# A two-block transformer in fp32 on one core: recombined feed-forward products with an addition done by DMA, unscaled rows at two norms, and another order of the chunks

## The chip, the cores and the metric

One core of one Trainium2 chip runs the whole program. The metric is the device time of one execution in microseconds (us). Before the change it is 2960.03 us, the median of three runs (2956.86 to 2961.02). A difference of about 0.2% (6 us) is what a measurement of this kernel can tell from none.

## What is computed

256 tokens of width 2048 go through two blocks, everything in fp32. The first has differential attention and a gated recurrence, cross attention, and a gated feed-forward part; the second has a pooling mixer and gated linear attention, and again a gated feed-forward part. The change lies in the two feed-forward parts, which are alike (5632 hidden columns):

```
def rms_norm(x, g):
    y = x * lax.rsqrt(jnp.mean(x * x, axis=-1, keepdims=True) + NORM_EPS)
    return y * g

h = rms_norm(x, ffn_pre_g)
gate, up = jnp.split(h @ w_ffn_in, 2, axis=-1)          # 2048 x 5632 each
x = x + rms_norm((silu(gate) * up) @ w_ffn_out, ffn_post_g)
```

The outputs must agree with this in fp32.

## The kernel before

**Weights.** The weights come from memory once, on SP's queue: `slab` (L378) loads two k-tiles of 128 rows by 512 columns, 512 KB, into one of six `raw` buffers. `parts` turns a slab into two reduced-precision halves that TensorE takes at full speed: ScalarE (ACT) casts it to `wh` (L386), VectorE (DVE) writes the rest `wl = raw - wh` (L387). There are eight pairs of such buffers. The activations h are held transposed in high and low parts as well, so a product is three matmuls per k-tile: high by high, high by low, low by high. The 256 tokens are two token tiles.

**A feed-forward part** has 11 hidden chunks of 512 columns, and `FF_ORDER` says in which order they run. `(c, False)` is a *plain* chunk: a group of matmuls for gate and one for up, 192 matmuls in all. `(c, True)` is a *fast* chunk (`seven`): gate and up of both token tiles as the four blocks of a matrix product that is done with seven block products instead of eight (P1, Q3, Q5, Q7, P2, Q6, Q4), 168 matmuls. It has four steps `s`. A step loads four slabs (x, b12, b22, b21), makes four sums of slabs on DVE (L490, L493, L495, L500) and splits seven things, so it has eleven DVE instructions of 128x1024 and seven casts on ACT, and gives TensorE 42 matmuls. The sums of h that the products need come from `combos` (8 additions L456, 8 further ones, and a split each, L449 on ACT and L450 on DVE); in the kernel before, these are spawned behind the first plain chunk, and so run at the start of the first fast one. After the last step the seven banks are combined (L512 to L519), then Silu and the product follow, and a transposition. `(a, b)` is a *down* stage: the hidden chunks a to b-1 times the down weights; all but the last one write partial sums through ACT (`yp`) and GpSimd's (POOL) DMA to `y_part` (L1065), the second and later ones accumulating there (L1067).

**The norm ahead of it** (`normed`, with `scaled=True` in both feed-forward parts): four sums of squares of a token tile's row, the reciprocal root, four scaled copies `xn` (L338), and only then the transposes (L309) and splits (L327, L328).

**The order.** Each engine runs its own queue in program order; the program places every instruction by a priority. Slabs and splits of a fast chunk go ahead by `SLAB_AHEAD` 70, the combining by `POST_AHEAD` 150; spawned work (norms, combos, transposes) is dealt out between the matmuls.

Of the kernel before, what the change touches and what calls it, by code (L numbers as in the profile page):

```python
# [41 lines left out]
FF_ORDER = ((0, False), (1, True), (0, 2), (2, True), (3, False), (4, True), (2, 5),  # L42
            (5, True), (6, False), (7, True), (5, 8), (8, True), (9, False), (10, True), (8, 11))
# [43 lines left out]
class Builder:  # L87
# [391 lines left out]
    def seven(self, Wa, Wb, c0, S, consume):  # L479
# [3 lines left out]
        bank = {n: self.psmm() if i < 4 else self.ps("mm7") for i, n in enumerate(("P1", "Q3", "Q5", "Q7", "P2", "Q6", "Q4"))}  # L483
        for s in range(4):
            with self.tc.high_priority(offset=max(0, min(SLAB_AHEAD, self.tc.cur_priority - self.base))):
                w = {}
                x = self.slab(Wa, 2 * s, c0)
                w["P1"] = self.parts(x)
                b12 = self.slab(Wb, 2 * s, c0)
                nc.vector.tensor_tensor(x, x, b12, ALU.add)  # L490
                b22 = self.slab(Wb, 8 + 2 * s, c0)
                w["Q3"] = self.parts(b22)
                nc.vector.tensor_tensor(b12, b12, b22, ALU.add)  # L493
                w["Q5"] = self.parts(x)
                nc.vector.tensor_tensor(x, x, b22, ALU.add)  # L495
                w["Q7"] = self.parts(b12)
                b21 = self.slab(Wa, 8 + 2 * s, c0)
                w["P2"] = self.parts(b21)
                w["Q6"] = self.parts(x)
                nc.vector.tensor_tensor(x, x, b21, ALU.add)  # L500
                w["Q4"] = self.parts(x)
            for n, (wh, wl) in w.items():
# [6 lines left out]
                self.tick()  # L509
        with self.tc.high_priority(offset=POST_AHEAD):  # L510
# [23 lines left out]
    def normed(self, start, pre, scaled=False):  # L534
# [5 lines left out]
        def job(t):  # L540
            self.bound = True
            if scaled:
                acc, xs = self.small(4, "acc"), []
                for j, u in enumerate(start(t)):
                    self.square_sum(u, acc[:, j:j + 1])
                    xs.append(u)
                s = self.small(1, "ssq")
                self.nc.vector.tensor_reduce(s, acc, AX.X, ALU.add)
                r = self.rsqrt_mean(s, D)
                for j in range(4):  # L550
                    u = self.unit(name="xn")
                    self.scaled_copy(u, xs[j], r)
                    xs[j] = u
            else:
                xs = list(start(t))
# [8 lines left out]
            if scaled:  # L564
                rstd[t] = r
                return
# [43 lines left out]
    def boundary(self, start, pre, scaled=False):  # L610
# [8 lines left out]
        rstd, hT, job = self.normed(first, pre, scaled)  # L619
        return xs, rstd, hT, job  # L620
# [240 lines left out]
    def block1(self, x_src):  # L861
# [120 lines left out]
        _, _, hT, job = self.boundary(self.spilled(done, xd), "ffn_pre_g", True)  # L982
# [8 lines left out]
        return self.ffn(xd, hT, W[:, :HID], W[:, HID:], A["w_ffn_out"][0], A["ffn_post_g"][0])  # L991
# [12 lines left out]
    def ffn(self, xd, hT, Wg, Wu, Wd, post):  # L1004
# [8 lines left out]
        def run(job):  # L1013
# [7 lines left out]
            def plain(c):  # L1021
                sg = [None] * NT
# [55 lines left out]
            for a, b in FF_ORDER:  # L1078
                if b is True:
                    fast(a)  # L1080
                elif b is False:
                    plain(a)
                    if S is None:
                        S, more = self.combos(hT)
                        self.spawn(more)
# [5 lines left out]
    def block2(self, ffn1):  # L1091
# [219 lines left out]
```

## Time and profile before

| | before |
| --- | --- |
| median of three runs | 2960.03 us |
| the profiled execution, its own time | 2953.59 us |
| its span (first to last instruction) | 2951.8 us |
| TensorE busy | 2811.8 us (95%) |
| DVE busy | 2132.8 us (72%) |
| ACT busy | 1602.5 us (54%) |
| the 14 fast stages together | 683.9 us |
| the other stages of the feed-forward parts | for example 44.6 to 46.2 us for a plain chunk |

A stage here is the stretch from TensorE's first matmul of a chunk to its last. In a fast stage TensorE waits again and again, in a plain one hardly. "Busy" of TensorE is modelled from pipelined matmuls: a 512-column matmul shows 0.39 us, but the next one starts 0.2257 us later.

### The profile page before, as it was taken

To read this page: it belongs to the slowest core of one execution; us is meant where nothing else is said; L and a number is where in the kernel's file an instruction comes from. 1 tells how busy PE (TensorE), PEld (TensorE's weight loads), DVE (VectorE), ACT (ScalarE), POOL (GpSimd) and SP (SyncE) were. 2 spreads that over 40 slices of the span, in tenths; PEclk is the share of its full clock that TensorE was granted. 3 is DMA by queue.
4 is the path that set the end of the run, shared out by engine and by line. 5 is a ranking of instruction groups with operands and counts; after the bars stand their busy time and mean duration, and the time that the engine had idled before them with its cause. 6 is when DMAs were issued, how large, how long until landed. Compare 5 with 4: busy or idle time off the path is not lost. (4 is left out here: it accounts for less than half of the span.)

```text
span 2951.8 us, 35680 instructions
## 1 busy us (share of the span) xinstructions
PE 2811.8 (95%) x12860; PEld 2287.3 (77%) x12860; DVE 2132.8 (72%) x2669; ACT 1602.5 (54%) x2342; POOL 98.7 (3%) x169
## 2 busy tenths in 40 slices
PE   8999999987999999999999999999988999999998
PEld 6788888875787777778888998888875777777777
DVE  7666685679887886887665575555569887887886
ACT  6555675675555545555555474444465555555553
POOL 1000000000000000000000000000000000000000
PEclk9999999999999999999999999999999999999999
DMA  8555555554557657657655556666654657557655
GB/s 254 171 175 160 178 176 176 169 167 143 191 190 238 168 168 229 218 184 247 206 154 162 153 169 205 200 195 219 202 168 125 207 193 229 158 186 233 198 189 183
DMA packets 285682, 556.16 MB, mean 188 GB/s; under 512 B 19049, under 2 KB 30949, under 8 KB 285504
## 3 DMA queue, kind: packets, MB, share of 16 engines
q1 hardware_dynamic: 271344, 516.89, 55.4%
q0 software_dynamic: 13584, 35.93, 4.8%
q8 instruction: 101, 1.65, 0.2%
q10 hardware_dynamic: 576, 1.05, 0.1%
q14 instruction: 77, 0.63, 0.1%
HBM read 531.25 MB, written 22.54 MB: 188 GB/s over the span
## 5 line engine op out<-in xcount | busy, mean ns | idle before, releaser
L387 DVE TENSOR_TENSOR wl<-raw,wh 128x1024 fp32r<-128x1024 f32 (+1 forms) x1136 | 1364.4, 1215 | 631.4 <-ACT wh L386 623.3
L386 ACT CAST wh<-raw 128x1024 fp32r<-128x1024 f32 (+1 forms) x1136 | 1170.6, 1046 | 1046.5 <-PE mm L418 580.5
L418 PE MATMUL mm<-wh,hi 128*128 128x512 f32 (+2 forms) x2608 | 827.2, 394 | 13.6 <-ACT wh L386 13.5
L418 PE MATMUL mm<-wl,hi 128*128 128x512 f32 (+2 forms) x2608 | 807.1, 389 | 0.9 <-DVE wl L387 0.9
L418 PE MATMUL mm<-wh,lo 128*128 128x512 f32 (+2 forms) x2608 | 803.5, 388 | 0.0
L418 PEld LDWEIGHTS mm<-wh,hi 128*128 128x128 f32 x2608 | 482.8, 188 | 114.6 <-ACT wh L386 17.9
L418 PEld LDWEIGHTS mm<-wh,lo 128*128 128x128 f32 x2608 | 489.3, 188 | 98.9 <-issue 0.2
L418 PEld LDWEIGHTS mm<-wl,hi 128*128 128x128 f32 x2608 | 488.4, 188 | 99.4 <-DVE wl L387 3.6
L506 PE MATMUL mm<-wh,sh 128*128 128x512 f32 x448 | 182.3, 407 | 48.1 <-ACT wh L386 30.4
L508 PE MATMUL mm<-wh,sl 128*128 128x512 f32 x448 | 175.9, 393 | 0.7 <-DVE sl L450 0.7
L507 PE MATMUL mm<-wl,sh 128*128 128x512 f32 x448 | 175.8, 392 | 0.0
L506 PE MATMUL mm<-wh,hi 128*128 128x512 f32 x336 | 137.2, 408 | 30.4 <-ACT wh L386 30.4
L506 PEld LDWEIGHTS mm<-wh,sh 128*128 128x128 f32 x448 | 84.5, 189 | 85.2 <-ACT wh L386 50.0
L507 PE MATMUL mm<-wl,hi 128*128 128x512 f32 x336 | 134.8, 401 | 3.0 <-DVE wl L387 2.9
L508 PE MATMUL mm<-wh,lo 128*128 128x512 f32 x336 | 132.7, 395 | 0.0
L433 PE MATMUL mm<-wh,hi 128*128 128x512 f32 (+1 forms) x304 | 121.4, 399 | 4.3 <-ACT hi L327 4.2
L435 PE MATMUL mm<-wh,lo 128*128 128x512 f32 (+1 forms) x304 | 119.2, 392 | 0.0
L434 PE MATMUL mm<-wl,hi 128*128 128x512 f32 (+1 forms) x304 | 119.2, 392 | 0.0
L506 PEld LDWEIGHTS mm<-wh,hi 128*128 128x128 f32 x336 | 63.8, 190 | 59.0 <-ACT wh L386 46.8
L508 PEld LDWEIGHTS mm<-wh,sl 128*128 128x128 f32 x448 | 84.6, 189 | 20.3 <-DVE sl L450 2.8
L507 PEld LDWEIGHTS mm<-wl,sh 128*128 128x128 f32 x448 | 84.7, 189 | 17.8
L328 DVE SCALAR_TENSOR_TENSOR lo<-tp,vec,hi 128x128 fp32r<-128x128 f32 x224 | 68.6, 345 | 20.9 <-ACT hi L327 20.1
(287 smaller groups left out, 2259.0 us busy)
## 6 DMA issues: line engine op xcount, KB each, us to landing
raw<-w_in SPq DMA_DIRECT2D x256, 512.0 KB, 3.7
raw<-w_ffn_in SPq DMA_DIRECT2D x176, 512.0 KB, 4.4
raw<-w_ffn_out SPq DMA_DIRECT2D x88, 512.0 KB, 5.4
raw<-w_ffn_gate SPq DMA_DIRECT2D x88, 512.0 KB, 4.3
raw<-w_ffn_up SPq DMA_DIRECT2D x88, 512.0 KB, 4.6
raw<-w_ffn_down SPq DMA_DIRECT2D x88, 512.0 KB, 5.4
raw<-w_out SPq DMA_DIRECT2D x64, 512.0 KB, 4.2
raw<-w_branch_b SPq DMA_DIRECT2D x32, 512.0 KB, 3.8
```

Of the source, the lines that this page charges most:

```text
L328: nc.vector.scalar_tensor_tensor(lo[:, i, :], ps[:, i, :], g, hi[:, i, :].bitcast(F32), ALU.mult, ALU.subtract)
L386: nc.scalar.copy(hi[:, :, :ncol], raw[:, :, :ncol])
L387: nc.vector.tensor_tensor(lo[:, :, :ncol], raw[:, :, :ncol], hi[:, :, :ncol].bitcast(F32), ALU.subtract)
L418: nc.tensor.matmul(ps[t][:, :ncol], hT[t][kk // 4][p][:, kk % 4, :], w[:, i, :ncol], start=kk == first and p == 0 and w is wh, stop=kk == ...
L433: nc.tensor.matmul(ps[:, :ncol], xh, wh[:, i, :ncol], start=kk == first, stop=False)
L434: nc.tensor.matmul(ps[:, :ncol], xh, wl[:, i, :ncol], start=False, stop=False)
L435: nc.tensor.matmul(ps[:, :ncol], xl, wh[:, i, :ncol], start=False, stop=kk == last)
L506: nc.tensor.matmul(bank[n], xh, wh[:, i, :], start=kk == 0, stop=False)
L507: nc.tensor.matmul(bank[n], xh, wl[:, i, :], start=False, stop=False)
L508: nc.tensor.matmul(bank[n], xl, wh[:, i, :], start=False, stop=kk == 7)
```

## The change

There are five things. **One**, in a fast step the addition b12 + b22 is no longer a DVE instruction but an accumulating DMA on POOL's queue from one SBUF buffer into another (512 KB); the other three sums stay on DVE (L511, L515, L517), and Q4's operand is now formed in b21's buffer. **Two**, the next step's x is loaded and split before Q4 of this one, and the products run in the order P1, Q3, Q5, P2, Q6, Q7, Q4. **Three**, the rows at the two feed-forward norms are transposed unscaled; the statistics are made afterwards, and the factor `rstd` is applied to the products, as Silu's scale and in a `scalar_tensor_tensor`. **Four**, `combos` is spawned between the gate and the up group of the first plain chunk, and two plain chunks run first. **Five**, `FF_ORDER`: still four plain and seven fast chunks, but five down stages in place of four, one of them of a single chunk, `(8, 9)`.

```diff
-FF_ORDER = ((0, False), (1, True), (0, 2), (2, True), (3, False), (4, True), (2, 5),
-            (5, True), (6, False), (7, True), (5, 8), (8, True), (9, False), (10, True), (8, 11))
+FF_ORDER = ((0, False), (1, False), (2, True), (0, 3), (3, True), (4, False), (5, True), (3, 6),
+            (6, True), (7, False), (8, True), (6, 8), (9, True), (8, 9), (10, True), (9, 11))
...
-        for s in range(4):
-            with self.tc.high_priority(offset=max(0, min(SLAB_AHEAD, self.tc.cur_priority - self.base))):
-                w = {}
-                x = self.slab(Wa, 2 * s, c0)
-                w["P1"] = self.parts(x)
-                b12 = self.slab(Wb, 2 * s, c0)
-                nc.vector.tensor_tensor(x, x, b12, ALU.add)
-                b22 = self.slab(Wb, 8 + 2 * s, c0)
-                w["Q3"] = self.parts(b22)
-                nc.vector.tensor_tensor(b12, b12, b22, ALU.add)
-                w["Q5"] = self.parts(x)
-                nc.vector.tensor_tensor(x, x, b22, ALU.add)
-                w["Q7"] = self.parts(b12)
-                b21 = self.slab(Wa, 8 + 2 * s, c0)
-                w["P2"] = self.parts(b21)
-                w["Q6"] = self.parts(x)
-                nc.vector.tensor_tensor(x, x, b21, ALU.add)
-                w["Q4"] = self.parts(x)
...
+        def early(s):
+            x = self.slab(Wa, 2 * s, c0)
+            return x, self.parts(x)
...
+        with ahead():
+            x, p1 = early(0)
+        for s in range(4):
+            with ahead():
+                w = {"P1": p1}
+                b12 = self.slab(Wb, 2 * s, c0)
+                b22 = self.slab(Wb, 8 + 2 * s, c0)
+                b21 = self.slab(Wa, 8 + 2 * s, c0)
+                nc.vector.tensor_tensor(x, x, b12, ALU.add)
+                nc.gpsimd.dma_start(b12, b22, accum_op=ALU.add)
+                w["Q3"] = self.parts(b22)
+                w["Q5"] = self.parts(x)
+                nc.vector.tensor_tensor(x, x, b22, ALU.add)
+                w["P2"] = self.parts(b21)
+                nc.vector.tensor_tensor(b21, b21, x, ALU.add)
+                w["Q6"] = self.parts(x)
+                w["Q7"] = self.parts(b12)
+                if s < 3:
+                    x, p1 = early(s + 1)
+                w["Q4"] = self.parts(b21)
+            products(s, ("P1", "Q3", "Q5", "P2", "Q6", "Q7", "Q4"), w)
...
-            if scaled:
-                acc, xs = self.small(4, "acc"), []
-                for j, u in enumerate(start(t)):
-                    self.square_sum(u, acc[:, j:j + 1])
-                    xs.append(u)
-                s = self.small(1, "ssq")
-                self.nc.vector.tensor_reduce(s, acc, AX.X, ALU.add)
-                r = self.rsqrt_mean(s, D)
-                for j in range(4):
-                    u = self.unit(name="xn")
-                    self.scaled_copy(u, xs[j], r)
-                    xs[j] = u
-            else:
-                xs = list(start(t))
+            xs = list(start(t))
...
-                    nc.scalar.activation(sg[t], ps, AF.Silu)
+                    nc.scalar.activation(sg[t], ps, AF.Silu, scale=rstd[t])
...
-                    nc.vector.tensor_tensor(u, ps, sg[t], ALU.mult)
+                    nc.vector.scalar_tensor_tensor(u, ps, rstd[t], sg[t], ALU.mult, ALU.mult)
...
                 self.group(Wg, c * CW, hT, ks, g_in, apart=c == 0)
+                if c == 0:
+                    S, more = self.combos(hT)
+                    self.spawn(more)
                 self.group(Wu, c * CW, hT, ks, u_in)
...
-                            nc.scalar.activation(g, g, AF.Silu)
-                            nc.vector.tensor_tensor(u, u, g, ALU.mult)
+                            nc.scalar.activation(g, g, AF.Silu, scale=rstd[t])
+                            nc.vector.scalar_tensor_tensor(u, u, rstd[t], g, ALU.mult, ALU.mult)
```

**DVE in a fast step.** Before, a step in the middle of a fast chunk stands like this on DVE (L490 to L500 are the four additions, L387 the low parts; `raw_7615` is x, `raw_7621` b12, `raw_7624` b22, `raw_7640` b21):

```order
L490 TENSOR_TENSOR raw_7615<-raw_7615,raw_7621 128x1024
L493 TENSOR_TENSOR raw_7621<-raw_7621,raw_7624 128x1024
L387 TENSOR_TENSOR wl_7632<-raw_7615,wh_7631 128x1024
L387 TENSOR_TENSOR wl_7637<-raw_7621,wh_7636 128x1024
L495 TENSOR_TENSOR raw_7615<-raw_7615,raw_7624 128x1024
L387 TENSOR_TENSOR wl_7643<-raw_7640,wh_7642 128x1024
L387 TENSOR_TENSOR wl_7647<-raw_7615,wh_7646 128x1024
L500 TENSOR_TENSOR raw_7615<-raw_7615,raw_7640 128x1024
L387 TENSOR_TENSOR wl_7652<-raw_7615,wh_7651 128x1024
L387 TENSOR_TENSOR wl_7700<-raw_7697,wh_7699 128x1024
L387 TENSOR_TENSOR wl_7709<-raw_7706,wh_7708 128x1024
L490 TENSOR_TENSOR raw_7697<-raw_7697,raw_7703 128x1024
```

In the changed kernel the same place reads (x is `raw_7328`, b12 `raw_7380`, b22 `raw_7382`, b21 `raw_7384`, the next step's x `raw_7410`):

```order
L511 TENSOR_TENSOR raw_7328<-raw_7328,raw_7380 128x1024
L387 TENSOR_TENSOR wl_7389<-raw_7382,wh_7388 128x1024
L387 TENSOR_TENSOR wl_7393<-raw_7328,wh_7392 128x1024
L387 TENSOR_TENSOR wl_7398<-raw_7384,wh_7397 128x1024
L515 TENSOR_TENSOR raw_7328<-raw_7328,raw_7382 128x1024
L517 TENSOR_TENSOR raw_7384<-raw_7384,raw_7328 128x1024
L387 TENSOR_TENSOR wl_7403<-raw_7328,wh_7402 128x1024
L387 TENSOR_TENSOR wl_7407<-raw_7380,wh_7406 128x1024
L387 TENSOR_TENSOR wl_7413<-raw_7410,wh_7412 128x1024
L387 TENSOR_TENSOR wl_7417<-raw_7384,wh_7416 128x1024
L511 TENSOR_TENSOR raw_7410<-raw_7410,raw_7462 128x1024
```

There are ten instructions between two first additions in place of eleven; the low part of Q7 (`wl_7407`, of the buffer that the DMA adds into) stands as the eighth, and the next step's P1 and Q4 stand behind it.

**SP's and POOL's queues.** In the changed kernel SP issues the four slabs of a step and the next ones like this; DMASW in the list of waits is a transfer of POOL's queue:

```order
L378 DMA raw_7380<-w_ffn_in 128x2x512 [waits DMAHW3_49,DVE_49]
L378 DMA raw_7382<-w_ffn_in 128x2x512 [waits DMASW0_49,DMAHW0_49,DVE_49,Activation_49]
L378 DMA raw_7384<-w_ffn_in 128x2x512 [waits DMAHW5_49,DVE_49,Activation_49]
L378 DMA raw_7410<-w_ffn_in 128x2x512 [waits DMAHW6_49,DVE_49]
L378 DMA raw_7462<-w_ffn_in 128x2x512 [waits DMAHW7_49,DVE_49]
L378 DMA raw_7464<-w_ffn_in 128x2x512 [waits DMASW2_49,DMAHW4_49,DVE_49,Activation_49]
```

and POOL, where a fast chunk follows a down stage, like this (L512 is the addition by DMA, L1069 the accumulation into `y_part`):

```order
L512 DMA raw_8736<-raw_8738 128x1024 [waits DMAHW3_49,DMAHW4_49,DMAHW2_49,DMAHW5_49,DMAHW1_49,DMAHW7_49,DMASW6_49,DVE_49]
L1069 DMA y_part_5590<-yp_8717 128x512 [waits DMASW7_49,Activation_49]
L512 DMA raw_8818<-raw_8820 128x1024 [waits DMAHW1_49,DMAHW0_49,DMAHW7_49,DMASW0_49,DVE_49]
L1069 DMA y_part_5594<-yp_8720 128x512 [waits DMASW1_49,Activation_49]
L512 DMA raw_8900<-raw_8902 128x1024 [waits DMAHW3_49,DMAHW4_49,DMASW2_49,DVE_49]
```

The slab b22 of each step now waits for the addition by DMA of an earlier step, and the slabs behind it on SP with it; before, no slab waited for POOL's transfers there, and POOL's queue held only the rows of `y_part`.

**The sums of h on DVE.** Before, they stand among the additions of the first fast chunk:

```order
L456 TENSOR_TENSOR sv_5994<-hi_5711,lo_5712 128x512
L456 TENSOR_TENSOR sv_5996<-hi_5753,lo_5754 128x512
L387 TENSOR_TENSOR wl_6160<-raw_6157,wh_6159 128x1024
L318 TENSOR_TENSOR lo_6009<-tp_5998,hi_6008 128x512
L318 TENSOR_TENSOR lo_6013<-tp_6003,hi_6012 128x512
L463 TENSOR_TENSOR sv_5996<-sv_5994,sv_5996 128x512
L490 TENSOR_TENSOR raw_6157<-raw_6157,raw_6163 128x1024
```

Now they stand among the low parts of the plain chunks' weights:

```order
L456 TENSOR_TENSOR sv_5828<-hi_5677,lo_5678 128x512
L456 TENSOR_TENSOR sv_5830<-hi_5719,lo_5720 128x512
L387 TENSOR_TENSOR wl_5877<-raw_5874,wh_5876 128x1024
L463 TENSOR_TENSOR sv_5830<-sv_5828,sv_5830 128x512
L387 TENSOR_TENSOR wl_6030<-raw_6027,wh_6029 128x1024
L450 TENSOR_TENSOR sl_5896<-sv_5830,sh_5895 128x512
```

They moved from the stage where DVE is nearly always busy into one where it is not.

## Rows read from the trace of the kernel before

**Rows 1.** The page, part 1: busy time, share of the span, instructions
```profile
PE 2811.8 (95%) x12860; PEld 2287.3 (77%) x12860; DVE 2132.8 (72%) x2669; ACT 1602.5 (54%) x2342; POOL 98.7 (3%) x169
```

**Rows 2.** TensorE's waits: what waited, for what; us in total, times, longest
```profile
PE mm L506 <- ACT wh L386: 60.8, 92, 0.9
PE mm L506 <- ACT sh L449: 17.7, 4, 7.4
```

**Rows 3.** Fast stages by window: us, busy of each engine, clock, DMA share, GB/s
```profile
661.30:721.70 60.40, 45.22 (x179) 32.52 (x177) 58.89 (x67) 30.92 (x36) 0.00 (x0) 0.94 0.37 115
...
972.80:1018.90 46.10, 40.63 (x170) 31.10 (x168) 42.39 (x39) 25.63 (x28) 1.72 (x2) 1.00 0.57 159
...
2219.50:2280.50 61.00, 46.39 (x179) 33.73 (x178) 59.49 (x68) 31.75 (x37) 0.00 (x0) 0.90 0.38 117
...
sum 683.90, PE 588.12 PEld 446.00 DVE 641.54 ACT 374.20 POOL 15.47; mean PE 42.01 PEld 31.86 DVE 45.82 ACT 26.73 POOL 1.11
```

**Rows 4.** A down stage, and a plain one behind a fast one, same columns
```profile
905.90:972.80 66.90, 66.48 (x297) 54.70 (x296) 45.04 (x43) 34.13 (x39) 5.29 (x6) 1.00 0.79 236
...
1226.20:1271.10 44.90, 44.83 (x201) 36.67 (x200) 35.32 (x35) 23.74 (x26) 2.72 (x5) 1.00 0.74 252
```

**Rows 5.** DVE's timeline in a fast stage: start, us, line, tiles [idle before]
```profile
990.74 1.22 DVE L490 TENSOR_TENSOR raw<-raw,raw 128x1024 f32<-128x1024 f32 x1
...
993.16 2.49 DVE L387 TENSOR_TENSOR wl<-raw,wh 128x1024 fp32r<-128x1024 f32 x2
...
999.23 1.23 DVE L500 TENSOR_TENSOR raw<-raw,raw 128x1024 f32<-128x1024 f32 x1
1001.65 3.50 DVE L387 TENSOR_TENSOR wl<-raw,wh 128x1024 fp32r<-128x1024 f32 x3 [1.19 <-ACT wh L386]
1005.06 1.22 DVE L490 TENSOR_TENSOR raw<-raw,raw 128x1024 f32<-128x1024 f32 x1
...
1016.03 1.22 DVE L387 TENSOR_TENSOR wl<-raw,wh 128x1024 fp32r<-128x1024 f32 x1
```

**Rows 6.** ACT's timeline in that step
```profile
1000.57 2.94 ACT L386 CAST wh<-raw 128x1024 fp32r<-128x1024 f32 x3 [2.63 <-DVE raw L500]
```

**Rows 7.** TensorE's timeline where that stage begins
```profile
972.60 0.39 PE L506 MATMUL mm<-wh,hi 128*128 128x512 f32 x1
972.82 0.39 PE L507 MATMUL mm<-wl,hi 128*128 128x512 f32 x1
```

**Rows 8.** TensorE's timeline at the two feed-forward norms: idle time before
```profile
608.70 3.68 PE L309 MATMUL tp<-ident,xn 128*128 128x128 f32 x16 [6.86 <-ACT xn L338]
...
630.60 0.50 PE L433 MATMUL mm<-wh,hi 128*128 128x512 f32 x1 [1.72 <-ACT hi L327]
...
2167.42 3.67 PE L309 MATMUL tp<-ident,xn 128*128 128x128 f32 x16 [6.15 <-ACT xn L338]
```

**Rows 9.** DVE's timeline there: the unscaled rows
```profile
597.40 2.73 DVE L600 SCALAR_TENSOR_TENSOR mg<-mg,r,mg 128x512 f32<-128x512 f32 x4
```

**Rows 10.** The window of the first of these transposes, columns as in rows 3
```profile
608.70:612.10 3.40, 3.40 (x17) 3.40 (x17) 1.37 (x5) 3.40 (x10) 0.00 (x0) 0.50 0.93 354
```

**Rows 11.** A group of instructions on DVE in the first fast stage: busy, mean ns
```profile
L450 DVE TENSOR_TENSOR sl<-sv,sh 128x512 fp32r<-128x512 f32 x8 | 5.5, 683 | 0.0
```

**Rows 12.** POOL's timeline: two accumulations into `y_part`, issued together
```profile
957.13 1.74 POOL L1067 DMA_DIRECT2D y_part<-yp  x2 [14.58 <-ACT yp L1063]
```

**Rows 13.** DMA issues of that pair, and of the pair at 925.5: KB each, median us to landing
```profile
y_part<-yp POOLq DMA_DIRECT2D x2, 256.0 KB, 4.9
...
y_part<-yp POOLq DMA_DIRECT2D x2, 256.0 KB, 8.4
```

**Rows 14.** All 32 accumulations of L1067, by line
```profile
DMA to landing us min/median/max: 3.9/5.8/9.2
```

**Rows 15.** DMA queues, 976.5 to 980.2: packets, MB, share of 16 engines
```profile
q0 software_dynamic: 288, 0.52, 78.2%
```

**Rows 16.** DMA issues of the first feed-forward part's slabs: KB each, median us to landing
```profile
raw<-w_ffn_in SPq DMA_DIRECT2D x176, 512.0 KB, 4.4
```

More of the change, by code (lines that the diff above doesn't have):

```diff
@@ L482, in seven, with products @@
         self.flush(lambda: all(None not in v for v in S.values()))
-        bank = {n: self.psmm() if i < 4 else self.ps("mm7") for i, n in enumerate(("P1", "Q3", "Q5", "Q7", "P2", "Q6", "Q4"))}
-        for s in range(4):
-            with self.tc.high_priority(offset=max(0, min(SLAB_AHEAD, self.tc.cur_priority - self.base))):
-                w = {}
-                x = self.slab(Wa, 2 * s, c0)
-                w["P1"] = self.parts(x)
-                b12 = self.slab(Wb, 2 * s, c0)
-                nc.vector.tensor_tensor(x, x, b12, ALU.add)
-                b22 = self.slab(Wb, 8 + 2 * s, c0)
-                w["Q3"] = self.parts(b22)
-                nc.vector.tensor_tensor(b12, b12, b22, ALU.add)
-                w["Q5"] = self.parts(x)
-                nc.vector.tensor_tensor(x, x, b22, ALU.add)
-                w["Q7"] = self.parts(b12)
-                b21 = self.slab(Wa, 8 + 2 * s, c0)
-                w["P2"] = self.parts(b21)
-                w["Q6"] = self.parts(x)
-                nc.vector.tensor_tensor(x, x, b21, ALU.add)
-                w["Q4"] = self.parts(x)
-            for n, (wh, wl) in w.items():
+        order = ("P1", "Q3", "Q5", "Q7", "P2", "Q6", "Q4")
+        bank = {n: self.psmm() if i < 4 else self.ps("mm7") for i, n in enumerate(order)}
+        def products(s, names, w):
+            for n in names:
+                wh, wl = w[n]
                 for i in range(2):
@@ L509, in seven, with ahead @@
                 self.tick()
+        def early(s):
+            x = self.slab(Wa, 2 * s, c0)
+            return x, self.parts(x)
+        def ahead():
+            return self.tc.high_priority(offset=max(0, min(SLAB_AHEAD, self.tc.cur_priority - self.base)))
+        with ahead():
[19 more added lines that the diff above has]
+            products(s, ("P1", "Q3", "Q5", "P2", "Q6", "Q7", "Q4"), w)
         with self.tc.high_priority(offset=POST_AHEAD):
@@ L532, in load_x, with normed @@
         return xs
-    def normed(self, start, pre, scaled=False):
+    def normed(self, start, pre):
         rstd, hT = [None] * NT, [[None] * 4 for _ in range(NT)]
@@ L563, in job @@
                 yield 1
-            if scaled:
-                rstd[t] = r
-                return
             acc = self.small(4, "acc")
@@ L608, in spilled, with boundary @@
         return f
-    def boundary(self, start, pre, scaled=False):
+    def boundary(self, start, pre):
         xs = [None] * NT
@@ L618, in first @@
                 yield u
-        rstd, hT, job = self.normed(first, pre, scaled)
+        rstd, hT, job = self.normed(first, pre)
         return xs, rstd, hT, job
@@ L981, in block1 @@
         xd = self.tc.dram_tile([T, D], F32, name="x_ffn1")
-        _, _, hT, job = self.boundary(self.spilled(done, xd), "ffn_pre_g", True)
+        _, rstd, hT, job = self.boundary(self.spilled(done, xd), "ffn_pre_g")
         with self.ahead():
@@ L990, in block1 @@
         W = A["w_ffn_in"][0]
-        return self.ffn(xd, hT, W[:, :HID], W[:, HID:], A["w_ffn_out"][0], A["ffn_post_g"][0])
+        return self.ffn(xd, rstd, hT, W[:, :HID], W[:, HID:], A["w_ffn_out"][0], A["ffn_post_g"][0])
     def chunks(self, W, hT, ks, cons, job):
@@ L1002, in chunks, with ffn @@
             self.group(W, n * CW, hT, ks, g, apart=n == 3)
-    def ffn(self, xd, hT, Wg, Wu, Wd, post):
+    def ffn(self, xd, rstd, hT, Wg, Wu, Wd, post):
         nc = self.nc
@@ L1021, in plain @@
             def plain(c):
+                nonlocal S
                 sg = [None] * NT
@@ L1082, in run @@
                     plain(a)
-                    if S is None:
-                        S, more = self.combos(hT)
-                        self.spawn(more)
                 else:
@@ L1234, in block2 @@
         xd = self.tc.dram_tile([T, D], F32, name="x_ffn2")
-        _, _, hT, job = self.boundary(self.spilled(done, xd), "norm_ffn_pre_2", True)
+        _, rstd, hT, job = self.boundary(self.spilled(done, xd), "norm_ffn_pre_2")
         self.chunks(A["w_out_2"][0], mT, ks, cons, job)
-        run, done = self.ffn(xd, hT, A["w_ffn_gate_2"][0], A["w_ffn_up_2"][0], A["w_ffn_down_2"][0],
+        run, done = self.ffn(xd, rstd, hT, A["w_ffn_gate_2"][0], A["w_ffn_up_2"][0], A["w_ffn_down_2"][0],
                              A["norm_ffn_post_2"][0])
```

## The prediction

> **What bounds the kernel now.** I read the busy shares first: TensorE 95% [rows 1]. So nearly every microsecond to be had is one in which TensorE waits, and TensorE's own work hardly changes (still four plain and seven fast chunks per feed-forward part). Then its waits [rows 2]: 60.8 us for the high parts `wh` of the fast products (92 waits, none over 0.9 us) and 17.7 us for the sums of h. Then the 14 fast stages by window [rows 3]: 683.9 us in all; the two first ones are 60.4 and 61.0, so the twelve others are 562.5, or 46.9 each. Next to them, the floor: matmuls follow each other at 972.82 - 972.60 = 0.22 us (0.2257 over a longer run), so 168 of them are 37.9 us. A fast stage is 9 us longer than its matmuls. In a plain stage TensorE is busy throughout, 44.83 of 44.90, with DVE at 35.3 [rows 4].
>
> Why 46.9: DVE. The step's first addition comes at 990.74 and the next one at 1005.06: 14.3 us per step against 42 x 0.2257 = 9.5 us of matmuls [rows 5]. Eleven instructions at about 1.19 (2.49 for two, less their overlap) are 13.1, and 1.19 is a wait: after the last addition (999.23) ACT begins its cast at 1000.57 [rows 6], and DVE can only go on at 1001.65. A fast stage starts with a full set of eight pairs, and then runs at DVE's pace. Its length is thus: 18.1 us from 972.60 to the third step's first addition, 14.3 to the fourth's, 11.0 from there to the low part of Q4 at 1016.03, its 1.2, and 1.35 for the last six matmuls: 46.0, as measured [rows 3, 5, 7].
>
> **The change part by part.** *One addition by DMA, other order.* DVE has ten instructions per step, 11.9 us, and the wait for a cast right behind an addition goes, since other low parts stand between. In its place stands a wait for the DMA. It is issued when L511 has read b12; Q7's cast on ACT waits for its landing, with the casts of the next P1 and of Q4 behind it in ACT's queue; DVE waits with Q7's low part, and behind that stand P1', Q4 and the next L511, which starts the next DMA. So a step takes the larger of 11.9 and 1.2 (L511) + A + 1.05 (cast) + 3 x 1.17 (Q7, P1', Q4) + about 0.3 of hand-overs = A + 6.05, where A is the time from issue to landing of a 512 KB addition. On SP, the next b22 waits for the same landing and holds up the slabs behind; it lands some 4.4 us after that [rows 16], about when the next step wants it, so it costs nothing as long as its load isn't much slower.
>
> A is not in the trace; accumulating transfers of 256 KB into memory are. Two of them issued together are as much data as one addition: issued 0.87 apart [rows 12], with a median landing of 4.9 [rows 13], they are done after about 5.8 to 6.6; by the median of all 32 it is 0.87 + 5.8 = 6.7 [rows 14]. In a crowded stretch a pair needs 0.9 + 8.4 = 9.3 [rows 13]. The low end: the fastest single one, 3.9 [rows 14], and the data of another 256 KB. Of the 288 packets in [rows 15], 256 carry data; 0.782 x 3.7 us x 16 / 256 = 181 ns each, so 128 more on 16 engines take 1.45: A = 5.4. I take A = 6.5, the middle of what the ordinary pairs show; a fast stage uses only about half of the DMA engines' time, 0.57 [rows 3]. The ends are 5.4 and 9.3.
>
> The shortest landing of 256 KB is 3.9 us [rows 14]. The Trainium skill ("DMA: Bandwidth & Descriptors", Anatomy of one DMA — SWDGE (gpsimd) path) gives 2.0 us plus bytes at 436 GB/s, an estimate of 3.2 us for 512 KB. By it DVE alone would set the step, and the whole would come out at about 2809 us on the timed runs. For half of the data it gives 2.6, where the rows show 3.9 at best and 5.8 in the median, so the trace does not agree with it for additions.
>
> The new stage: the first slab pair comes free after six matmuls (1.35), the cast takes 1.05, so Q3's low part of the second step can begin at 2.4; nine instructions later, and 0.9 for hand-overs, the third step's L511 starts at 14.0. Then P, then P - 1.2 to Q4's end, and 1.65 for the last hand-over and six matmuls: 14.45 + 2P, or 26.55 + 2A. With A = 6.5 it is 39.6; I take **40**, 2 over the floor of 37.9. A = 5.4 gives 38.4. From A = 8 on the second step's addition is late too, and the stage is 18.5 + 3A.
>
> *Twelve later fast stages*: 562.5 - 12 x 40 = **-82**. *Two first fast stages*: they hold 24 more instructions for the sums of h, 16.4 us (0.683 each) [rows 11], and waits of up to 7.4 for them [rows 2]. With these gone they are like the others: 121.4 - 80 = **-41**.
>
> *The sums of h* go among the two plain chunks, 86.8 us of matmuls. DVE has there 32 low parts (38 us), the sums (16.4), the first fast step (12) and some five more: 71, so they fit. But DVE's queue is in order and they stand ahead of low parts that TensorE wants soon; zero to 4 each, I take 2: **+4**.
>
> *Unscaled rows.* TensorE stands still for 6.86 and 6.15 us for `xn` and 1.72 for a split [rows 8]; the transposes behind that run at a granted clock of 0.50, the lower of the two levels, 1.2 GHz [rows 10]: 16 in 3.7 us. The unscaled rows are ready at 600.1 [rows 9], and TensorE stops only 6.9 us ahead of 608.70, at about 601.8, so the first wait goes. The statistics then run beside the gate group; ACT needs them before its first Silu, 48 matmuls or 11 us later. At most 6.9 + 1.7 + 1.7 (half of the slow transposes' time), at least 5; I take 9 each: **-18**. What is late next is the splits L327 and L328 of each tile, which follow the transposes as now.
>
> *Five down stages.* The down stage of one chunk has only 96 matmuls, 21.7 us; DVE has its 8 low parts (9.5), the combining of the fast chunk ahead (7.5) and the first step of the next one (11 to 13): 28 to 30. The shortfall is up to 8, part of which is made up earlier; I take 4 each: **+8**. Another 8 copies and 8 accumulations per feed-forward part go beside the matmuls on ACT (54% busy) and POOL (3%) [rows 1]: **+2** for both parts. On POOL an L1069 that waits for its copy stands ahead of an L512, as the order shows; the copy follows TensorE by under 1 us and the L512 is wanted later, so nothing for that.
>
> Sum: -82 - 41 + 4 - 18 + 8 + 2 = **-127**, against the profiled execution's 2953.6: 2827. The runs shown have a median 6 us above that execution, so I say **2832**.
>
> **The rivals.** *The addition is slow* (A = 7.5 to 9.3): the DMA engines are shared with the slabs, and the source and the target both lie in SBUF, which no row shows. For it: the pair with 8.4 [rows 13]; against it: the DMA share of a fast stage, 0.37 to 0.57 [rows 3], against 0.79 where that pair ran [rows 4]. At A = 8.3 a stage is 43.5: 14 x 3.5 = +49 on the forecast, 2881. Chance 0.18.
>
> *The fast stage's end takes over.* The combining after the stage (seven DVE instructions) frees the banks for the next stage later, as the product order puts Q7 next to last. 4 us at each of 14 stages is +56: 2888. Against it: plain stages behind a fast one start without a wait now [rows 4]. Chance 0.08.
>
> *The fast stages don't shorten*, because ACT or the slabs set the pace there and not DVE: then only the norms and the sums of h are left, -18 - 28 + 14 = -32, 2928. Against it: DVE is 42.4 of 46.1 busy, ACT 25.6 [rows 3]. Chance 0.04.
>
> *Slower than before*: the same loop through the DMA, but with A above the break-even. 14 stages of f us against 683.9, with -18 and +14 beside, break even at f = 49.1, that is 18.5 + 3A, A = 10.2. At A = 11, f is 51.5: +33, 2993. For it: 9.2 is the longest of 32 landings of half the data [rows 14], and a queue of slabs ahead on the same engines adds to it. Against it: the pairs at 5.8 to 6.7. Chance 0.06, and 0.03 for a time within 0.2%.
>
> **How the numbers follow.** The forecast (A up to 7.5) has 0.61; its own range is 2795 to 2860. The low end of all: A = 5.4 (-22), norms 2 better each and none of the +14: 2792. The high end takes in the slow addition and the late banks: 2895. About 0.15 is left out, most of it above. Faster by over 0.2%: 0.91; within 0.2%, about what a measurement of this kernel can tell from none: 0.03; slower: 0.06.
>
> **What would show it.** In the profile after: fast stages of 39 to 42 us, the two first ones like the rest; L511 to L511 12 to 13 us; landings of L512's transfers at 5.4 to 7.5; the wait for `xn` gone, and a clock near 1 at the transposes. The forecast is wrong if the landings are above 8, if TensorE waits for Q7's `wh` by more than 2 us per step, or if the stages behind the fast ones have got longer by what these gave.

## The result, and the profile after

| | before | after |
| --- | --- | --- |
| median | 2960.44 us (2956.86 to 2961.02) | 2842.11 us (2840.42 to 2844.20) |
| ratio, 95% interval | | 0.9603 (0.9586 to 0.962) |
| span of the profiled execution | 2951.8 us | 2840.9 us |

It is faster by 118 us; 2832 was forecast, in 2792 to 2895. The page of the kernel after, part 1, answers to [rows 1]: TensorE was 95% busy and is 98%.

```profile
PE 2781.8 (98%) x12860; PEld 2282.2 (80%) x12860; DVE 2061.9 (73%) x2613; ACT 1605.2 (57%) x2344; POOL 162.4 (6%) x241
```

TensorE's waits after, against [rows 2]: the 60.8 us for `wh` of the fast products and the 17.7 us for the sums of h are gone, and nothing of that size stands in their place.

```profile
PE mm L493 <- DVE wl L387: 7.4, 11, 0.8
PE tp L309 <- DVE e L1043: 7.3, 8, 2.1
PE mm L418 <- DVE e L529: 5.0, 6, 0.9
...
PE mm L492 <- ACT yp L1065: 3.7, 2, 2.1
```

Windows of the kernel after, columns as in [rows 3]: the first fast stage, an ordinary one, the down stage of one chunk and the fast stage behind it, the second part's first fast stage, its tenth chunk, and the last down stage.

```profile
697.40:736.70 39.30, 39.30 (x177) 31.92 (x175) 38.92 (x37) 26.37 (x28) 2.60 (x3) 1.00 0.71 193
888.10:927.20 39.10, 39.10 (x178) 32.01 (x176) 38.91 (x37) 26.34 (x28) 2.60 (x3) 1.00 0.70 194
...
1201.50:1227.40 25.90, 23.56 (x106) 18.48 (x105) 23.41 (x25) 14.81 (x19) 6.19 (x7) 1.00 0.91 256
1227.40:1274.30 46.90, 42.32 (x171) 32.11 (x169) 39.74 (x36) 27.00 (x29) 10.87 (x17) 0.96 0.89 251
2196.20:2236.80 40.60, 39.88 (x178) 31.87 (x176) 39.02 (x37) 26.32 (x28) 2.60 (x3) 1.00 0.69 191
...
2734.40:2780.40 46.00, 41.06 (x171) 31.07 (x170) 39.82 (x36) 27.02 (x29) 10.85 (x17) 1.00 0.90 255
2780.40:2831.20 50.80, 46.87 (x199) 36.62 (x199) 34.53 (x48) 22.63 (x34) 0.00 (x0) 0.97 0.53 197
```

The first fast stage went from 60.4 to 39.3 and an ordinary one to 39.1, where the twelve before had a mean of 46.9; TensorE is busy throughout. The two fast stages of the tenth chunk are the exception: 46.9 and 46.0. Of the 14 fast stages, twelve are 38.1 to 40.6 us, and 469 together.

That is nearly TensorE's own work. In a stretch without waits, 36 matmuls of this trace follow each other 0.2267 us apart, not 0.2257:

```profile
603.83 0.39 PE L433 MATMUL mm<-wh,hi 128*128 128x512 f32 x1
...
611.99 0.39 PE L433 MATMUL mm<-wh,hi 128*128 128x512 f32 x1
```

So 168 matmuls are 38.1 us (192 are 43.5, 288 are 65.3), and the eight transposes that run in a fast stage behind a plain chunk add about 1.2. The twelve stages lie 0.4 us above that in the mean.

DVE's timeline in an ordinary stage after, against [rows 5]:

```profile
902.89 1.22 DVE L511 TENSOR_TENSOR raw<-raw,raw 128x1024 f32<-128x1024 f32 x1
904.03 3.64 DVE L387 TENSOR_TENSOR wl<-raw,wh 128x1024 fp32r<-128x1024 f32 x3
...
910.00 4.63 DVE L387 TENSOR_TENSOR wl<-raw,wh 128x1024 fp32r<-128x1024 f32 x4
914.55 1.22 DVE L511 TENSOR_TENSOR raw<-raw,raw 128x1024 f32<-128x1024 f32 x1
```

One step takes 914.55 - 902.89 = 11.66 us where it took 14.3, and no idle time is shown in it. So on DVE its ten instructions fill the step, and it doesn't wait for the DMA. (ACT does, at 23 of the 56 additions, 29.6 us in all.) The 56 additions by DMA landed in (line L512 of the trace, min, median, max):

```profile
DMA to landing us min/median/max: 4.5/5.4/8.5
```

At the norm, TensorE's timeline has in place of the standstill of 6.86 us and of transposes at half clock [rows 8, 10] transposes among matmuls at a granted clock of 1.00, the higher of the two levels, 2.4 GHz (window 616.3 to 619.1), and one wait of 0.94, the only one for `mg` at the two norms:

```profile
616.36 1.32 PE L309 MATMUL tp<-ident,mg 128*128 128x128 f32 x8 [0.94 <-DVE mg L598]
617.81 0.60 PE L309 MATMUL tp<-ident,mg 128*128 128x128 f32 x4
```

Four transposes take 0.60 us; of the 16 before, four took 0.92.

### The profile page after: what moved, and what is told of

Same layout as the page of the kernel before. It is cut to its first block, busy times and chain, and to the rows that moved or that the text cites. A ratio compares the mean times of both kernels' runs of the same rounds, so it can differ in the third digit from the quotient of the medians.

```text
span 2840.9 us, 35858 instructions
## 1 busy us (share of the span) xinstructions
PE 2781.8 (98%) x12860; PEld 2282.2 (80%) x12860; DVE 2061.9 (73%) x2613; ACT 1605.2 (57%) x2344; POOL 162.4 (6%) x241
## 5 line engine op out<-in xcount | busy, mean ns | idle before, releaser
L387 DVE TENSOR_TENSOR wl<-raw,wh 128x1024 fp32r<-128x1024 f32 (+1 forms) x1136 | 1360.4, 1214 | 604.7 <-ACT wh L386 599.0
L418 PE MATMUL mm<-wh,hi 128*128 128x512 f32 (+2 forms) x2624 | 828.4, 393 | 9.9 <-DVE e L529 5.0
L418 PE MATMUL mm<-wl,hi 128*128 128x512 f32 (+2 forms) x2624 | 818.8, 391 | 3.0 <-DVE wl L387 2.6
L418 PE MATMUL mm<-wh,lo 128*128 128x512 f32 (+2 forms) x2624 | 815.7, 389 | 0.0
L418 PEld LDWEIGHTS mm<-wh,hi 128*128 128x128 f32 x2624 | 485.8, 188 | 113.4 <-DVE e L529 7.5
L418 PEld LDWEIGHTS mm<-wl,hi 128*128 128x128 f32 x2624 | 491.5, 188 | 104.2 <-DVE wl L387 7.9
L418 PEld LDWEIGHTS mm<-wh,lo 128*128 128x128 f32 x2624 | 491.8, 188 | 99.3 <-DVE lo L318 1.3
L492 PE MATMUL mm<-wh,sh 128*128 128x512 f32 x448 | 175.5, 392 | 4.1 <-ACT yp L1065 3.7
L433 PE MATMUL mm<-wh,hi 128*128 128x512 f32 (+1 forms) x288 | 114.6, 398 | 1.7 <-ACT hi L327 1.4
L434 PE MATMUL mm<-wl,hi 128*128 128x512 f32 (+1 forms) x288 | 113.2, 393 | 0.3 <-DVE wl L387 0.2
L435 PE MATMUL mm<-wh,lo 128*128 128x512 f32 (+1 forms) x288 | 112.7, 392 | 0.4 <-DVE lo L328 0.4
L512 POOL DMA_DIRECT2D raw<-raw x56 | 51.3, 917 | 741.7 <-DVE raw L511 324.4
L327 ACT ACTIVATE hi<-tp,vec 128x128 fp32r<-128x128 f32 x224 | 72.7, 383 | 12.4 <-DVE lo L328 7.3
```

What stands on the lines that cost most here:

```text
L327: nc.scalar.activation(hi[:, i, :], ps[:, i, :], AF.Copy, scale=g)
L387: nc.vector.tensor_tensor(lo[:, :, :ncol], raw[:, :, :ncol], hi[:, :, :ncol].bitcast(F32), ALU.subtract)
L418: nc.tensor.matmul(ps[t][:, :ncol], hT[t][kk // 4][p][:, kk % 4, :], w[:, i, :ncol], start=kk == first and p == 0 and w is wh, stop=kk == ...
L433: nc.tensor.matmul(ps[:, :ncol], xh, wh[:, i, :ncol], start=kk == first, stop=False)
L434: nc.tensor.matmul(ps[:, :ncol], xh, wl[:, i, :ncol], start=False, stop=False)
L435: nc.tensor.matmul(ps[:, :ncol], xl, wh[:, i, :ncol], start=False, stop=kk == last)
```

## The experiments

The kernel before ran beside each of them and had medians from 2955 to 2957; ratios are against it. Windows and timelines are of one execution of each kernel; of e2, e3 and e5 there is one execution at all, of e10 there are two.

**One part undone or alone.** e1 puts the addition back on DVE:

```diff
-                nc.gpsimd.dma_start(b12, b22, accum_op=ALU.add)
+                nc.vector.tensor_tensor(b12, b12, b22, ALU.add)
```

> The changed kernel with one part undone: b12 + b22 is a DVE instruction again (eleven per step), the order within the step, the norms, the sums of h and FF_ORDER stay as changed. Theory (the number of DVE instructions sets the step: 11.66 us with ten in the changed kernel): 11 x 1.17 = 12.8 us per step, a fast stage of 2.4 + 11.7 + 0.9 + 12.8 + 11.7 + 1.65 = 41.2 in place of 39.2, so +24 on the twelve ordinary stages; the two fast stages before the last down stage, which wait for the DMA, lose that wait, about -10. Time 2850 to 2862. Rival 1 (the new order within the step did it all, DVE has slack): 2836 to 2848. Rival 2 (the addition is all of the gain, the order gives nothing): stages of 46.9 again, 2930 to 2945.

Measured: 2851.41, ratio 0.9645 (0.9629 to 0.9661), so slower than the changed kernel by 9 us in the medians and by 0.42% or 12 us in the ratios. Two ordinary stages, the down stage of one chunk, and the fast one behind it:

```profile
891.80:935.70 43.90, 41.74 (x178) 33.10 (x177) 43.51 (x42) 26.93 (x29) 0.00 (x0) 0.96 0.45 149
1001.90:1042.10 40.20, 39.00 (x170) 31.41 (x168) 40.06 (x37) 26.14 (x29) 1.72 (x2) 1.00 0.58 164
1214.40:1240.00 25.60, 23.23 (x105) 18.64 (x105) 24.32 (x26) 16.27 (x21) 5.28 (x6) 1.00 0.89 244
1240.00:1287.30 47.30, 42.18 (x170) 32.31 (x169) 43.34 (x40) 27.00 (x30) 8.22 (x14) 0.96 0.80 258
```

The theory on DVE holds in the ordinary stages (40 to 44; both rivals are out, the first more clearly by the stages than by the time). One step of it fell: the fast stage behind the short down stage is 47.3 without any DMA addition, so the landing alone doesn't make that stage long. It isn't the same 47, though: here casts wait in it for slabs (up to 4.9 us), in the changed kernel for additions (up to 3.1); e7 decides.

The 12 us are also what is left when a larger gain and a loss are set against each other. The 14 fast stages together, e1 and then the changed kernel:

```profile
sum 593.60, PE 563.95 PEld 449.10 DVE 583.96 ACT 369.44 POOL 25.49; mean PE 40.28 PEld 32.08 DVE 41.71 ACT 26.39 POOL 1.82
sum 562.10, PE 549.78 PEld 443.79 DVE 533.41 ACT 367.14 POOL 62.49; mean PE 39.27 PEld 31.70 DVE 38.10 ACT 26.22 POOL 4.46
```

The twelve plain and down stages between them, in the same order:

```profile
sum 589.20, PE 581.70 PEld 476.33 DVE 449.97 ACT 308.88 POOL 38.01; mean PE 48.48 PEld 39.69 DVE 37.50 ACT 25.74 POOL 3.17
sum 599.10, PE 586.16 PEld 477.23 DVE 443.27 ACT 313.69 POOL 48.81; mean PE 48.85 PEld 39.77 DVE 36.94 ACT 26.14 POOL 4.07
```

The last down stage of each part in e1, and the first part's in the changed kernel (the second part's, 50.80, is above):

```profile
1287.20:1333.80 46.60, 45.51 (x201) 36.35 (x199) 37.57 (x50) 26.26 (x39) 0.00 (x0) 1.00 0.79 263
2795.90:2842.70 46.80, 45.52 (x201) 36.34 (x199) 33.63 (x47) 20.45 (x32) 0.00 (x0) 1.00 0.49 173
...
1274.30:1326.20 51.90, 47.18 (x199) 36.81 (x199) 38.74 (x51) 28.48 (x42) 0.00 (x0) 0.97 0.81 279
```

So the addition by DMA gains 31.5 us in the fast stages and costs 9.9 in the stages between them and 9.3 in the two last ones.

e2 issues the DMA twice:

> The changed kernel with the accumulating DMA issued twice, the second one when the first has landed (so Q7 multiplies b12 + 2 b22: that part of the result is not the reference's). Theory (the loop through the DMA is the larger of DVE's 11.7 and A + 6.05): A goes from 5.4 to about 11, the step to 17 us and the fast stage to 18.5 + 3 x 11 = 51, against 39.2: +160, about 3000 us, with ACT waiting for the DMA in every step. Rival (the landing is hidden well enough that one more addition is hidden too): within 10 us of 2842.

Measured: 3060.79, slower than the 3000 expected, because the two additions one behind the other took 12.3 us and not 11. ACT's timeline shows the wait, and DVE's the step:

```profile
1054.47 2.95 ACT L386 CAST wh<-raw 128x1024 fp32r<-128x1024 f32 x3 [6.47 <-DMA raw<-raw]
```

```profile
1040.95 1.23 DVE L511 TENSOR_TENSOR raw<-raw,raw 128x1024 f32<-128x1024 f32 x1
...
1055.56 3.50 DVE L387 TENSOR_TENSOR wl<-raw,wh 128x1024 fp32r<-128x1024 f32 x3 [5.16 <-ACT wh L386]
1058.97 1.22 DVE L511 TENSOR_TENSOR raw<-raw,raw 128x1024 f32<-128x1024 f32 x1
```

From the first L511's end (1042.18) to the cast's start is 12.3 us, and the step is 18.0; A + 6.05 gives 18.35. So the loop L511, addition, Q7's cast, Q7, P1', Q4 is what the prediction said, and the landing is hidden by little: with A = 5.4 the loop is 11.45, against DVE's 11.66. Twice costs 219 us, 15.6 for each fast stage.

e3 is the addition by DMA alone, in the kernel before:

```diff
-                nc.vector.tensor_tensor(b12, b12, b22, ALU.add)
+                nc.gpsimd.dma_start(b12, b22, accum_op=ALU.add)
```

> The kernel before with one part alone: b12 + b22 by DMA, in the old order, where Q7 is split third and six more DVE instructions of the step stand behind it. Theory (where the wait stands in DVE's queue decides): L490 1.2, issue 0.4, landing 5.4, cast 1.05, seven DVE instructions 8.2 and the wait for Q4's cast 1.2 make a step of 17.4 us against 14.3 before: fast stages some 6 to 9 us longer, 3040 to 3080 us. Rival (an instruction less on DVE counts wherever the DMA stands): a step of 13.1, stages 2 to 3 us shorter, 2920 to 2935.

Measured: 3067.13, some 110 us slower than the kernel before. DVE's timeline:

```profile
1015.03 1.22 DVE L490 TENSOR_TENSOR raw<-raw,raw 128x1024 f32<-128x1024 f32 x1
1017.44 1.23 DVE L387 TENSOR_TENSOR wl<-raw,wh 128x1024 fp32r<-128x1024 f32 x1 [1.19 <-ACT wh L386]
...
1022.28 3.50 DVE L387 TENSOR_TENSOR wl<-raw,wh 128x1024 fp32r<-128x1024 f32 x3 [2.36 <-ACT wh L386]
...
1028.23 3.50 DVE L387 TENSOR_TENSOR wl<-raw,wh 128x1024 fp32r<-128x1024 f32 x3 [1.19 <-ACT wh L386]
1031.64 1.22 DVE L490 TENSOR_TENSOR raw<-raw,raw 128x1024 f32<-128x1024 f32 x1
```

A step of 16.6 with one instruction less and 4.7 us of waits; before, it had 1.2 of waits [rows 5]. The additions landed in 4.6 here (median), with which the expected sum of 17.4 becomes 16.6. Taking work off the bound engine lost time, because the wait for it stood early in that engine's queue.

e10 is the order within the step alone, in the kernel before:

> The kernel before with one part alone: the new order within a fast step (next x split ahead, Q4 in b21's buffer, products in the new order), the addition still on DVE, everything else as before. Theory (the old order makes DVE wait for the cast behind its last addition and holds Q4 up at the end of the stage; e1's ordinary stages were 40.3 to 44.1, 41.6 in the mean): 12 x (46.9 - 41.6) = 64 and about 5 at each of the two first stages, so 2957 - 74 = 2883, 2870 to 2895. Rival (order and addition by DMA only work together): above 2935.

Measured: 2887.41, ratio 0.9764 (0.9744 to 0.9783): -69 us, as the theory has it. Its ordinary stages are 40.3 to 44; one of them:

```profile
852.20:894.60 42.40, 40.56 (x178) 31.85 (x176) 42.33 (x41) 25.94 (x29) 0.00 (x0) 1.00 0.47 148
```

Of the two halves of the fast step, the order is the larger in the whole: 69 us by itself. The addition by DMA brings about 12 more on top of it (31.5 in the fast stages alone, by e1), and loses 110 without it.

e4 scales the rows at the norms again:

```diff
-            xs = list(start(t))
+            if scaled:
+                acc, xs = self.small(4, "acc"), []
+                for j, u in enumerate(start(t)):
+                    self.square_sum(u, acc[:, j:j + 1])
...
```

> The changed kernel with one part undone: at the two feed-forward norms the rows are scaled before their transposes again, and Silu and the product take no factor. Theory (TensorE's standstill of 6.9 and 6.2 us, the split's 1.7 and the slow transposes come back): +14 to +20, 2856 to 2862. Rival (the statistics only moved into the first plain chunk, whose Silu then waits as long): within 5 us of 2842.

Measured: 2860.49, ratio 0.9678 (0.9664 to 0.9693): 18 us in the medians, 0.75% or 22 us in the ratios. The rival is out. TensorE's waits have the standstill back:

```profile
PE tp L309 <- ACT xn L338: 14.0, 3, 6.9
```

e5 spawns the sums of h behind the second plain chunk:

```diff
-                if c == 0:
-                    S, more = self.combos(hT)
-                    self.spawn(more)
...
                     plain(a)
+                    if a == 1:
+                        S, more = self.combos(hT)
+                        self.spawn(more)
```

> The changed kernel with one part undone: the sums of h are spawned behind the second plain chunk, so they run at the start of the first fast one, as in the kernel before. Theory (DVE is full in a fast stage and has room in the plain ones): 16.4 us of DVE and the wait for the first sums come back into two stages, 55 to 58 us each in place of 39.5 and 40.8: +31 to +37, 2873 to 2880. Rival (they cost the plain chunks nearly as much): under +15, below 2857.

Measured: 2883.61 in one execution, 41 us slower and so a little more than the 31 to 37 expected. The first fast stage is 56.6 (39.3 with the sums in the plain chunks), DVE full:

```profile
697.30:753.90 56.60, 45.75 (x177) 33.65 (x177) 55.09 (x63) 31.33 (x37) 2.60 (x3) 0.91 0.52 142
```

The stretch ahead of it, both plain chunks included, ends at the same time as in the changed kernel (697.3 against 697.4): the sums cost those chunks nothing that can be seen.

**The order of the chunks.** e6 has the old `FF_ORDER`:

> The changed kernel with FF_ORDER of the kernel before (one plain chunk ahead of the first fast one, four down stages); the sums of h then lie in the only plain chunk ahead. Theory (a short or late down stage starves the engines beside it): the single-chunk down stage and the fast stage behind it give back 2 x 11.8, the last down stage with three chunks in place of two 2 x 6; against that DVE has 16.4 + 9.5 + 12 = 38 us of work in the 21.7 us of the first plain chunk's second group, +10 to +16 at each of two places: 2824 to 2840. Rival (the single-chunk stage's cost is something else and the two plain chunks ahead matter more): above 2848.

Measured: 2845.68, ratio 0.9626 (0.9611 to 0.9641), which lies between the two expectations: the first fast stage is 52.8, 13.5 more than after, as expected, but the last down stage, with three chunks, is 74.9 where the theory had it get better. So the new order of the chunks, as it stands, is worth 0.2% (4 us in the medians, 7 in the ratios), with intervals that overlap: not told from nothing.

e7 and e8 cut the down stages differently:

```diff
-FF_ORDER = ((0, False), (1, False), (2, True), (0, 3), (3, True), (4, False), (5, True), (3, 6),
-            (6, True), (7, False), (8, True), (6, 8), (9, True), (8, 9), (10, True), (9, 11))
+FF_ORDER = ((0, False), (1, False), (2, True), (0, 2), (3, True), (4, False), (5, True), (2, 4),
+            (6, True), (7, False), (8, True), (4, 6), (9, True), (6, 8), (10, True), (8, 11))
```

(this is e8; e7 has (0, 3), (3, 5), (5, 7), (7, 9), (9, 11).)

> The changed kernel with the down stages cut 3, 2, 2, 2, 2 in place of 3, 3, 2, 1, 2. Theory (a down stage of one chunk is too short for the work that DVE, ACT and POOL have in it): its 4.4 us, and the 7 us by which the fast stage behind it is longer than the others, go, at two places: 2842 - 23 = 2819, 2814 to 2826. Rival (it is the tenth fast chunk's place, close ahead of the end, not the length of the stage ahead of it): within 6 us of 2842.

> The changed kernel with the down stages cut 2, 2, 2, 2, 3. Theory: as with 3, 2, 2, 2, 2, and the last stage has two chunks of matmuls (not one) ahead of the transposes of the tenth chunk that TensorE waited for, 5 to 6 us each: 2842 - 23 - 11 = 2808, 2802 to 2818. Rival (the wait at the last stage isn't cover but the reload of y_part and x): the same as with 3, 2, 2, 2, 2, about 2819.

Measured: e7 2829.78, ratio 0.9569 (0.9552 to 0.9586); e8 2826.61, 0.9559 (0.9544 to 0.9574). Windows of e7: the down stage that now has two chunks, the tenth chunk, the last down stage.

```profile
1182.10:1228.80 46.70, 45.13 (x202) 36.71 (x201) 36.00 (x37) 26.28 (x31) 6.13 (x7) 1.00 0.93 272
1228.80:1268.10 39.30, 38.57 (x170) 31.27 (x168) 36.62 (x33) 24.62 (x26) 10.92 (x17) 1.00 0.88 243
2764.50:2818.70 54.20, 47.72 (x201) 37.12 (x199) 35.58 (x50) 23.35 (x35) 0.92 (x2) 0.97 0.54 194
```

The tenth chunk went from 46.9 to 39.3, which settles it: the short down stage is the cause, and the DMA share, 0.88 against 0.89, is not. DVE's timelines show how. The tenth chunk's second step begins 5.9 us behind the stage's start in the changed kernel (1227.40) and 0.25 ahead of it in e7 (1228.80):

```profile
1233.31 1.22 DVE L511 TENSOR_TENSOR raw<-raw,raw 128x1024 f32<-128x1024 f32 x1
...
1228.55 1.23 DVE L511 TENSOR_TENSOR raw<-raw,raw 128x1024 f32<-128x1024 f32 x1
```

Of these 5.9 us, 2.9 are a wait for the cast behind the first addition, which is issued 7.2 us ahead of the stage (1220.21) and cast from 1228.81 on. In e7 it is issued 15 us ahead (1213.78), and no cast waits for it. But only about 10 to 13 of the 23 us were gained. The down stage ahead is still 3.2 above its matmuls (46.7 against 43.5), where 25.9 against 21.8 was 4.1. Another part of the rest is in the last down stage, 50.8 before and 54.2 now, where 192 matmuls are 43.5; in e8 it has 288 matmuls and 72.4 us, where the kernel before needed 66.8:

```profile
2744.10:2816.50 72.40, 68.88 (x297) 55.43 (x295) 45.74 (x58) 31.48 (x43) 0.00 (x0) 0.98 0.60 211
```

**The last down stage.** In e8 its first slabs landed late (DMA issues of 2738 to 2749: count, KB, median us to landing), against 4.3 for six of them in the kernel before:

```profile
raw<-w_ffn_down SPq DMA_DIRECT2D x7, 512.0 KB, 10.0
```

POOL's queue holds the re-reads of `y_part` (L1055) behind the last addition by DMA, so that they run just ahead of these slabs and beside them:

```profile
2731.91 0.88 POOL L512 DMA_DIRECT2D raw<-raw  x1 [11.10 <-DVE raw L511]
2732.45 4.13 POOL L1055 DMA_DIRECT2D y<-y_part  x7
```

In the window of the slabs above, 2.71 of the 4.09 MB moved are the software queue's, which is POOL's. In e1, which has no addition by DMA, the re-reads are issued from 2755.37 on, 40 us ahead of its last stage. e9 takes e8, moves the re-reads to SP's queue, and loads x with the last group:

```diff
-                            y[t][n] = self.unit(name="y")
-                            nc.gpsimd.dma_start(y[t][n], yd[t][n])
...
                 for n in range(4):
                     if last:
+                        for t in range(NT):
+                            y[t][n] = self.unit(name="y")
+                            nc.sync.dma_start(y[t][n], yd[t][n])
```

> The kernel with down stages 2, 2, 2, 2, 3 and one thing more: in the last down stage the partial sums y_part are read back on SP's queue, two per group of matmuls, and x behind the last group's slabs, not all at its start on POOL's queue behind the last addition by DMA. Theory (4 MB of re-reads that the additions hold back until the last fast stage's end collide with the slabs of the last down stage, whose landing went from about 4 to 10 us): the 7 us that TensorE loses there, in two places, mostly go: 2827 - 12 = 2815, 2808 to 2820. Rival (the slabs are late because their buffers come free late): within 4 us of 2827.

Measured: 2824.18, ratio 0.955 (0.9534 to 0.9566): 0.1% better than e8, inside the intervals. The slabs land in 6.6 and the stage is 69.7, so in the traces the re-reads (with x, which moved too) explain some 2.7 of 5.6 us there; as a cause of the whole the theory fell. That the slabs' buffers come free late wasn't tested by itself.

e11 takes e9 and puts the addition of the tenth chunk alone back on DVE:

> The kernel of e9 with one thing more: in the last fast chunk of each feed-forward part (the tenth) the addition is on DVE, in the others by DMA. Theory (what is left of the last down stage's loss, 69.8 us against 66.8 before, comes from the additions in the fast stage ahead: they hold back SP's slabs and use the DMA engines): the last down stage falls to 67, the fast stage ahead rises from 39.7 to 41 to 42, so the whole moves by -3 to 0: 2821 to 2824. Rival (the loss is the combining of the tenth chunk, which now ends with Q4 and has one chunk of cover less time): the last down stage stays at 70 and the whole is 2824 to 2828.

Measured: 2819.94, ratio 0.9535 (0.9523 to 0.9548), the fastest of all. The tenth chunk and the last stage:

```profile
2700.60:2740.80 40.20, 39.00 (x170) 31.39 (x168) 40.06 (x37) 25.91 (x28) 3.95 (x6) 1.00 0.67 194
2740.80:2808.90 68.10, 66.92 (x297) 54.41 (x295) 44.95 (x57) 30.08 (x41) 0.00 (x0) 1.00 0.64 228
```

The stage is 68.1. Against e9 the whole moved by 0.15%, which the intervals don't separate. That the additions have a part in the last stage's loss is shown by e1 and e10 instead, which have the new order within the step and no addition by DMA: 46.6 and 46.8 in e1 against 51.9 and 50.8 with the same down stages, and 67.4 in e10, next to 66.8 before. The rival of e11's expectation, the later combining of the tenth chunk, would have kept these stages long as well, so it isn't the main cause. How the additions' part divides between the re-reads that they hold up and the DMA engines' time is not separated beyond e9 and e11. The last 1.3 us of e11 stay open.

## Why the prediction came out

**The step.** Right, with the size of A at the lower end: landings of 5.4 in the median, where 6.5 was taken. With A = 5.4 the prediction had DVE's 11.9 us as the larger term and a stage of 38.4 (its formula, 14.45 + 2P, gives 38.25); measured were 11.66 and, without the tenth chunks, 39.1 in the mean (469 us over 12). Here TensorE's own 38.1 to 39.3 is the larger term, since 14.45 + 2 x 11.66 is 37.8: the floor of 37.9 was taken too low, with 0.2257 per matmul and without the transposes. The rule from the data of two `y_part` transfers was too high: one addition of 512 KB takes 5.4 here, a single 256 KB in [rows 14] 5.8. The two differ in size and in target (SBUF, memory), and no run separates these.

The formula of the Trainium skill ("DMA: Bandwidth & Descriptors", Anatomy of one DMA — SWDGE (gpsimd) path), 2.0 us plus the bytes at 436 GB/s, gives an estimate of 3.2 us for 512 KB. The fastest of 56 took 4.5, so the trace doesn't agree with it for these transfers; DVE's step would be the same with either.

**The fast stages.** -123 was forecast for all (-82 and -41). Measured: 683.9 to 562 (469 + 46.9 + 46.0), -122. That agreement has two errors in it that cancel: twelve stages are 0.9 better than 40 (-11), and the two tenth chunks 6 to 7 worse (+13). There is luck in the whole, too: with the A that was measured, the prediction's own sum would have been 22 us lower, 2810, and 32 below the time. A landing taken too long stood in for costs outside the fast stages that were left out.

**The norms.** -18 forecast, 18 to 22 measured by e4 (medians, ratios). Mechanism and size were right.

**The sums of h.** -41 for their leaving the two first fast stages, which went from 121.4 to 79.9; e5 brings back 17.3 at the first of them. Their price in the plain chunks was +4 in the sum and can't be seen in e5.

**The short down stage.** +8 for both was the term with the right mechanism and too small a size: the two fast stages behind are 7 to 8 longer than the others, and the stages themselves are 25.9 for 21.8 us of matmuls. Half of DVE's shortfall was said to be made up earlier; DVE came 5.9 us late into the tenth chunk, and e7, where it doesn't, has stages of 39.3 there.

**Not in the sum at all:** what the additions cost outside the fast stages, 19 us by the comparison with e1. About half lies in the last down stage: 50.8 for 192 matmuls (43.5), against 66.8 for 288 (65.3) before, so 5.8 more there. The prediction passed over POOL's queue with "nothing for that"; the re-reads behind it weren't looked at. The late slabs are part of it (e9). The other half lies in the stages behind the fast ones.

**The rivals.** A slow addition: ruled out by the landings; e2 shows its price. The banks at the stage's end: the wait of L418 for L529 is 5.0 us in all, not 56; it is there, 0.9 at a time, as are 7.3 us in which transposes wait for the product that follows the combining (L1043). In e1 the first of these waits is not there, and the plain and down stages are 9.9 us shorter. This rival is thus a part of the 16 us by which the span fell short of the forecast (-110.9 against -127), beside the last down stages. The fast stages not shorter: out. Slower than before: e3 shows how near that mechanism lies, with A no slower (4.6 in the median) but the wait in another place of the queue.

## What to carry to other kernels

Work that goes from a full engine to a DMA queue pays only if the wait for it stands late enough in that engine's queue: the same edit lost 110 us in the old order and gained about 12 in the new one, and the order by itself gained 69. Add up all stages before you call it a gain: of 31.5 us in the fast stages, 19 were lost beside them. Write the loop down as a sum (instruction, landing, cast, instructions that stand behind) and compare it with the engine's own work per step. When a bound is removed in the stages, look at once at the shortest stage between them and at the last one: what feeds the next stage had its time there.

## What the runs showed that was not expected

An accumulating DMA from SBUF to SBUF of 512 KB landed in 5.4 us in the median (4.5 at best, 8.5 at worst), no slower than 256 KB into memory (5.8). 56 of them raised the DMA share of the ordinary fast stages to 0.69 to 0.82, where e1 has 0.44 to 0.58, with TensorE busy nearly throughout; what they cost was paid in the stages beside.
